# Two of four delta heads turned by VectorE and small stores in place of TensorE; output weights placed in attention's slots

## The chip, the cores and the metric

The kernel is one program on 1 core of one Trainium2 chip, launched once. Its time is the device time of that core in microseconds (us). Five engines work side by side, each through a queue of its own in a fixed order: PE (TensorE, matrix products; PEld is its weight load), DVE (VectorE), ACT (ScalarE), POOL (GpSimd) and SP (SyncE, which here issues nearly all DMAs). An instruction that waits holds everything behind it in its own queue.

## The reference, cut to what matters

One decoder block over 1024 tokens of width 1024, in float32: RMSNorm, one input projection, two groups of heads side by side, one output projection with the residual, and a last RMSNorm.

```python
h = rmsnorm(x, norm1_w)
proj = einsum('btd,de->bte', h, w_in)
sb_q, sb_k, sb_v, sb_z, g_q, g_k, g_v, g_z, g_b, g_a = split(proj)
o_sb = rmsnorm(stick_breaking_attention(sb_q, sb_k, sb_v)) * silu(sb_z)      # 8 heads of 64
qkv = silu(causal_depthwise_conv(concat([g_q, g_k, g_v]), conv_w))           # 4 taps
gq, gk, gv = split(qkv); gq = l2norm(gq); gk = l2norm(gk)                    # 4 heads of 128
o_gdn = gated_delta_chunked(gq, gk, gv, decay, beta)
o_gdn = rmsnorm(o_gdn) * silu(g_z)
x = x + einsum('bte,ed->btd', concat([o_sb, o_gdn]), w_out)
return rmsnorm(x, final_norm_w)
```

Stick-breaking attention weighs an earlier key s with sigmoid(z_ts) times the product of (1 - sigmoid) over the keys between. The gated delta rule works in chunks: inside a chunk a triangular system is solved, and a 128x128 state is carried from chunk to chunk (kernel: chunks of 128 tokens).

## The kernel before, in words

**Products.** Float32 accuracy comes from three products of split operands: each operand is a high part plus a low part (`xh`, `xl`; `weh`, `wel`; `woh`, `wol`; `mh`, `ml`), and `mm3` adds high x high, high x low, low x high. ScalarE makes the high part of a weight, GpSimd (for the output weights VectorE) the low part.

**Order.** The program isn't written in its order. Generators (streams) hand out pieces of work, and a model of the engines inside the builder (`Model`, with a `cost` for each instruction) decides at build time in which order each queue gets them; the five queues are then fixed. A DMA's cost in that model is a count of contiguous runs times a price per run. So an edit of one cost or one stream can move instructions in all queues.

**Stages.** Loads and the normalised input come first; then q of attention, half of v and the decays. Then the streams run together until about 520 us. `projections` goes through 16 column groups in the order G0 v1 k0 G1 k1 G2 k2 G3 k3 z4 to z7 z0 to z3: G is a delta head's k, q and v, z a gate. A group is 2 halves of 512 tokens with 24 products each; its products fill PE where the others leave room. `attention` goes through 8 heads with 4 windows each: products `pz<-kh,q`, sigmoids, a scan, `sgf` tiles, which PE transposes (`pz<-step,stf`), then `po<-ahl,v2a`. The windows' tiles lie in four fixed places, `sg0` to `sg3`.

**Delta heads.** `g_evac` takes a projected half of k (kind 1), q (kind 0) or v (kind 2): a copy to `pre`, four conv taps, sigmoid and product into `ac` (128 channels x 512 tokens), and a store to `g_s` in DRAM. `delta_load` loads k and q together as `kq` and v as `vt`, all with channels on the partitions. `gdn_pre` needs k, q and v with tokens on the partitions too: PE transposes them in blocks of 128x128 (`pz<-step,kwf`: k and q, 8 for each half of a head; `pz<-step,vt`: v, 4), ScalarE sums the squares of k and q (`nkv<-pz`), VectorE copies k to `kn`, ScalarE scales v into `nkv`. Then come the products of k with k and q (`pz<-kqf`), the triangular inverse (`gdn_sub`, `gdn_inv`) and the scan over chunks (`gdn_chain`), whose first product is `pc<-nkv,xinv`.

**Output.** When the delta heads are done, their pool is closed and the pool `f0` opened over it; eight row blocks of the output weights are loaded (`wor`) and split, the delta half (4 to 7) in `f0`, attention's half (0 to 3) in `f1` over the projection's pool. `enter_delta` and `enter_attention` load the mixed rows (`mgf`), `split` transposes and splits them (`mf`, `mh`, `ml`), and the last products go to `pp`.

**How to read names.** All instructions have line L358 (a helper records them), so rows are told apart by their tiles: out<-in. Numbers at the end of a tile are buffer numbers.

Of the kernel before, what the change touches and what calls it, by code (L numbers as in the profile page):

```python
# [28 lines left out]
ORDER = "G0 v1 k0 G1 k1 G2 k2 G3 k3 z4 z5 z6 z7 z0 z1 z2 z3".split()  # L29
LOADS = "k0 k1 x0 k2 x1 x2 k3 x3 x4 k4 x5 k5 x6 x7 k6 k7 c0 c1 c2 c3 s c4 c5 c6 c7".split()  # L30
WINDOWS = 3

# [360 lines left out]
def cost(eng, name, args, kw):  # L393

    size = lambda ap: int(np.prod(ap.shape[1:]))
    n = size(args[0])
    if eng == "S":
        run = min(contiguous(args[0]), contiguous(args[1]))
        return max(60, int(np.prod(args[0].shape)) * 4 / run * (10 + run / 21) / 16)
    if eng == "P":  # L400
        if name == "transpose":
            return 58 if args[1].dtype == F32R else 108
        n = size(args[2])
        if args[2].dtype == F32R:
# [69 lines left out]
def block(tc, xT_d, x_d, n1_d, wE_d, wQ_d, wC_d, conv_d, alog_d, dtb_d, mixw_d, wo_d, fnw_d, out_d):  # L474
# [4 lines left out]
    with ExitStack() as top:  # L479
# [391 lines left out]
        def g_evac(h, kind):  # L871
            wv = conv[:, 4 * kind + h, :]
            last = []

            def evac(pt, half):
                pre = gd.tile([P, 515], F32, tag="pre", bufs=2, name="pre")
                if half == 0:
                    V.memset(pre[:, 0:3], 0.0)
                else:
                    A.activation(pre[:, 0:3], last[0][:, 512:515], AF.Copy)  # L880
                last.append(pre)
                first(A.activation, pre[:, 3:515], pt, AF.Copy)
# [95 lines left out]
        def delta_load():  # L978
            yield lambda: "dec" in flags
            for h in range(GH):  # L980
                for g in range(2):
                    u = 2 * h + g
                    gst[h, g] = {}
                    half = "" if g else ".0"
                    yield lambda: u < 4 or f"c{u - 4}" in flags
                    if u > 3:
                        yield flags[f"c{u - 4}"]
                    kq = fx.tile([P, 4, 2, P], F32, "kq", "kq")
                    ts = slice(512 * g, 512 * g + 512)
# [4 lines left out]
                    gst[h, g].update(kq=kq)  # L994
                    flags[f"l{u}g"] = loads
                    yield lambda: f"G{h}2{half}" in flags and (u == 0 or f"q{u - 1}" in flags)
                    vt = gd.tile([P, 4, P], F32R, tag="vt", name="vt")
# [24 lines left out]
        def gdn_pre(h, g):  # L1022
            st = gst[h, g]
            kq = st["kq"]
            cs = slice(4 * g, 4 * g + 4)
            kn = gd.tile([P, 4, P], F32, tag="kn", bufs=4, name="kn")
# [6 lines left out]
            nkv = gd.tile([P, 4, P], F32, tag="nkv", bufs=4, name="nkv")  # L1033
            kw = fx.words(kq, "kw")
            for which in range(2):
# [5 lines left out]
                sq = [("A", 250)] * 4  # L1041
# [14 lines left out]
            G.tensor_scalar(qe, ss[:, 1, :], EPS * P, None, ALU.mult)  # L1056
            yield r
            nm = dt
            at = gd.tile([P, 4, P], F32, tag="at", bufs=4, name="at")
            for i in range(2):  # L1060
                gpt = pz()
                for j in range(2):
# [10 lines left out]
            flags[f"p{2 * h + g}"] = r  # L1073
            yield from until(f"v{2 * h + g}g")
            vt = st["vt"]
            tp = pz()
            for j in range(4):
                TE.transpose(tp[:, j * P:(j + 1) * P].bitcast(F32R), vt[:, j, :], idr)
            for j in range(4):
                A.activation(nkv[:, j, :], tp[:, j * P:(j + 1) * P], AF.Copy, scale=nk[:, j:j + 1])  # L1080
# [305 lines left out]
        wts = {}  # L1386
        pools = {}

        def weights_of(pool, ks, tag, bufs):
            ks = list(ks)  # L1390
            raws = {}

            def load(k):
                r = pool.tile([P, D], F32, tag=tag, bufs=bufs, name="wor")
                raws[k] = r, S.dma_start(r, wo_d[k * P:(k + 1) * P, :])

            for k in ks[:2]:
                load(k)
            for n, k in enumerate(ks):
                w, landed = raws[k]  # L1400
                yield landed
                wh, wl = [pool.tile([P, D], F32R, name=f"wo{c}{k}") for c in "hl"]
                A.activation(wh, w, AF.Copy, scale=mixw[:, k:k + 1])
                wts[k] = wh, wl, V.scalar_tensor_tensor(wl, w, mixw[:, k:k + 1], wh.bitcast(F32), ALU.mult, ALU.subtract)
                if n + 2 < len(ks):
                    load(ks[n + 2])

        def out_weights():
            yield lambda: "g" in flags
            gdn_ctx.close()  # L1410
            pools[0] = open_pool("f0", before=gd.ops())
            flags["pool0"] = True
            yield from weights_of(pools[0], range(4, 8), "xr", 3)

        def out_weights_attention():
# [4 lines left out]
            yield from weights_of(pools[1], range(4), "wr", 2)  # L1420
# [23 lines left out]
            return pools[0].tile([P, D], F32, tag="xr", bufs=3, name=name) if b < 3 else pools[1].tile([P, D], F32, tag="yr", bufs=5, name=name)  # L1444

        def enter_delta():
            yield lambda: "pool0" in flags and "z7" in flags and len(wts) > 1
            f0 = pools[0]
            for b in range(NB):
                yield lambda: fx.room("kq")  # L1450
# [82 lines left out]
        def products_attention():  # L1533
            yield lambda: f"d{NB - 1}" in flags
            for b in range(NB):
# [3 lines left out]
                for got in product(b, 0, parts):  # L1539
# [43 lines left out]
        pre = Stream(delta_pre(), 0.7, DELTA + 0.7)  # L1583
        interleave(ck, lambda: ps.room("pz", 4),
                   [Stream(delta_scan(), 0, DELTA), Stream(delta_solve(), 0.5, DELTA + 0.5), Stream(delta_substitute(), 0.6, DELTA + 0.6),
                    pre, Stream(delta_load(), 0.4, DELTA + 0.4), Stream(attention(), 9.995, WINDOW), Stream(attention_values(), 9.99, WINDOW), Stream(out_weights(), 9, OUT_WEIGHTS), Stream(out_weights_attention(), 9.25, OUTPUT + 1), Stream(enter_x(), 9.31, OUTPUT), fill,
                    Stream(enter_delta(), 9.3, OUTPUT), Stream(prepare(1), 9.2, OUTPUT), Stream(products_delta(), 101, OUTPUT),
                    Stream(enter_attention(), 9.1, OUTPUT - 3), Stream(prepare(0), 9.05, OUTPUT - 2), Stream(products_attention(), 102, OUTPUT - 1.5)])

# [37 lines left out]
```

## Time and profile before

| | |
|---|---|
| time, median of 3 runs | 645.64 us (645.34 to 646.01) |
| profiled execution, its own time | 647.36 us |
| its span (first to last instruction) | 645.0 us |
| TensorE's granted clock, mean | 0.998 |
| mean DMA rate over the span | 173 GB/s |

The span is shorter than the execution's own time, since starting and ending lie around it. The profile's page gives each engine's busy time and its share of the span, the chain of work that ended last, groups of instructions (count, busy us, mean ns of one, idle time of the engine before them and what ended it), and DMA issues (count, KB each, median us from issue to landing). Queries of the trace give the instructions in order of time (start us, length us), waits by engine (total us, times, longest), and busy times by window.

### The profile page before, as it was taken

What the parts mean: (1) busy time and instruction counts of PE and PEld (TensorE: products, weight loads), DVE (VectorE), ACT (ScalarE), POOL (GpSimd) and SP (SyncE); (2) the same over time, 40 slices, a digit from 0 to 9 for tenths busy, and PEclk for the clock granted to TensorE, in tenths of its full rate; (3) what the DMA queues carried; (4) which work ended last, traced back from release to release, by engine and by line L of the source; (5) the groups of instructions that cost most, each with busy time, mean ns of one, the idle gap of its engine ahead of it and who ended that gap; (6) DMA issues with size and microseconds to landing.
All of it is one profiled execution on the core that took longest, in us unless ns stands there. A gap on an engine that the chain in (4) does not pass through costs nothing.

```text
span 645.0 us, 11378 instructions
## 1 busy us (share of the span) xinstructions
PE 633.7 (98%) x3816; PEld 540.5 (84%) x3816; DVE 435.6 (68%) x810; ACT 392.6 (61%) x943; POOL 340.6 (53%) x429
## 2 busy tenths in 40 slices
PE   8999999999999999999999999999999999999996
PEld 7889988988888888888888788888888887888785
DVE  4359985133776797776877677667869527486874
ACT  5665467553876677856877766757578533222653
POOL 0125142964978487773569596477626131224742
PEclk9999999999999999999999999999999999999999
DMA  8968235886286352656254583444512259962323
GB/s 294 303 245 305 86 131 162 313 286 229 81 262 189 99 172 81 202 182 185 71 169 125 158 274 84 123 146 117 185 52 73 79 191 332 357 197 65 99 99 130
DMA packets 96633, 111.80 MB, mean 173 GB/s; under 512 B 28544, under 2 KB 61504, under 8 KB 96576
## 3 DMA queue, kind: packets, MB, share of 16 engines
q1 hardware_dynamic: 96288, 110.89, 52.2%
q8 instruction: 30, 0.49, 0.3%
q14 instruction: 27, 0.22, 0.1%
q10 hardware_dynamic: 288, 0.20, 0.1%
HBM read 76.03 MB, written 35.03 MB: 172 GB/s over the span
## 4 chain that ended last, share of the span: by engine, by line
PE 53%; POOL 3%; issue 2%; DVE 2%; DMA 1%; ACT 0%; POOLq 0%; SPq 0%
PE pp L358 34%; PE pz L358 13%; PE po L358 4%; PE pc L358 2%; DMA vt<-g_s 1%; POOL sgf L358 1%; POOL rsb L358 1%; POOL tt L358 0%; DVE xr L358 0%; POOL ac L358 0%; DVE cc L358 0%; POOL wel L358 0%; DVE ahl L358 0%; POOL ml L358 0%; POOL ry L358 0%
## 5 line engine op out<-in xcount | busy, mean ns | idle before, releaser
L358 PE MATMUL pp<-xh,weh 128*128 128x512 f32 x360 | 146.0, 406 | 0.0
L358 PE MATMUL pp<-xh,wel 128*128 128x512 f32 x360 | 141.2, 392 | 0.0
L358 PE MATMUL pp<-xl,weh 128*128 128x512 f32 x360 | 140.5, 390 | 0.0
L358 POOL TENSOR_TENSOR sgf<-sgf,cc 128x128 f32<-128x128 f32 (+3 forms) x64 | 77.3, 1210 | 48.0 <-DVE cc L358 46.7
L358 POOL TENSOR_TENSOR wel<-wer,weh 128x512 fp32r<-128x512 f32 x48 | 62.1, 1298 | 68.2 <-ACT weh L358 66.4
L358 PEld LDWEIGHTS pp<-xh,wel 128*128 128x128 f32 x360 | 67.5, 188 | 15.1
L358 PEld LDWEIGHTS pp<-xl,weh 128*128 128x128 f32 x360 | 67.8, 188 | 11.7
L358 PEld LDWEIGHTS pp<-xh,weh 128*128 128x128 f32 x360 | 67.7, 188 | 11.6
L358 DVE TENSOR_TENSOR_SCAN cc<-pz,step 128x384 f32<-128x384 f32 (+2 forms) x64 | 53.4, 847 | 13.7 <-ACT pz L358 7.5
L358 DVE TENSOR_TENSOR ahl<-pz,ahl 128x512 fp32r<-128x512 f32 (+1 forms) x80 | 50.0, 631 | 11.9 <-ACT ahl L358 11.5
L358 ACT ACTIVATE ahl<-pz 128x512 fp32r<-128x512 f32 (+1 forms) x80 | 44.0, 563 | 17.7 <-PE pz L358 17.4
L358 ACT ACTIVATE sgf<-pz,rs 128x384 f32<-128x384 f32 (+3 forms) x96 | 52.9, 593 | 1.5 <-PE pz L358 1.1
L358 PE MATMUL pp<-woh,mh 128*128 128x512 f32 (+2 forms) x132 | 52.1, 395 | 1.2 <-DVE xr L358 1.2
L358 ACT ACTIVATE pz<-pz,ns 128x384 f32<-128x384 f32 (+3 forms) x96 | 52.2, 577 | 0.0
L358 PE MATMUL pp<-woh,ml 128*128 128x512 f32 (+2 forms) x132 | 50.9, 385 | 0.0
L358 PE MATMUL pp<-wol,mh 128*128 128x512 f32 (+2 forms) x132 | 50.6, 384 | 0.0
L358 PE MATMUL po<-ahl,v2a 128*128 128x512 f32 (+1 forms) x160 | 49.0, 401 | 0.0
L358 POOL TENSOR_TENSOR ac<-ac,pre 128x512 f32<-128x512 f32 x24 | 30.9, 1291 | 30.8 <-ACT pre L358 24.2
L358 POOL TENSOR_TENSOR ml<-mf,mh 128x512 fp32r<-128x512 f32 x16 | 22.0, 1377 | 42.6 <-ACT mh L358 32.3
L358 DVE SCALAR_TENSOR_TENSOR pp<-pre,conv,pp 128x512 f32<-128x512 f32 x42 | 31.5, 749 | 18.3 <-ACT pp L358 18.0
L358 DVE TENSOR_TENSOR_SCAN cc<-pz,cc,step 128x512 f32<-128x512 f32 (+1 forms) x32 | 38.8, 1211 | 5.5 <-ACT pz L358 4.8
L358 PE MATMUL pz<-kh,q 128*128 128x384 f32 (+3 forms) x96 | 36.0, 381 | 0.2 <-DVE cc L358 0.2
(290 smaller groups left out, 1531.5 us busy)
## 6 DMA issues: line engine op xcount, KB each, us to landing
wer<-wE SPq DMA_DIRECT2D x48, 256.0 KB, 3.0
xr<-x SPq DMA_DIRECT2D x16, 512.0 KB, 7.4
g_s<-ac SPq DMA_DIRECT2D x24, 256.0 KB, 2.1
v_s<-v2e SPq DMA_DIRECT2D x16, 256.0 KB, 3.0
kqf<-g_s SPq DMA_DIRECT2D x16, 256.0 KB, 3.4
v2a<-v_s SPq DMA_DIRECT2D x8, 512.0 KB, 5.9
q<-qk_s SPq DMA_DIRECT2D x8, 512.0 KB, 4.0
kh<-qk_s SPq DMA_DIRECT2D x8, 512.0 KB, 3.9
```

The costliest lines, as they stand in the source:

```text
L358: ins = f(*args, **kw).ins
```

## The change

It has four parts.

1. For delta heads 2 and 3 (`h >= TURNED`), `g_evac` lets VectorE transpose the 128x512 result in blocks of 32x32 into the first 512 columns of `pre`, and stores that as four pieces of 32 partitions, in runs of 128 bytes, to a new array `gt_s`, whose rows are tokens. k and q are stored to `g_s` as well, v isn't.
2. For these heads `delta_load` loads `kn` (k), `nkv` (q) and `vt` (v) from `gt_s`, with tokens on the partitions; `gdn_pre` squares and scales from these tiles. PE's transposes and the copy to `kn` are left out. Heads 0 and 1 stay as they were.
3. The output weights' rows are loaded into the places `sg2` and `sg3`, two at a time, from attention's last windows on. Blocks 4 to 7 are split into attention's slots (`kh`, `kl`, `q2`, `cc`, `v2a`, `ahl`), blocks 0 to 3 in `f0`.
4. The builder's price for one DMA run of r bytes goes from 10 + r / 21 to 7.5 + r / 23.4 ns. This alone can move instructions anywhere.

```diff
+TURNED = 2
-        return max(60, int(np.prod(args[0].shape)) * 4 / run * (10 + run / 21) / 16)
+        return max(60, int(np.prod(args[0].shape)) * 4 / run * (7.5 + run / 23.4) / 16)
...
+        gt_s = dr.tile([GH, 3, T, P], F32, name="gt_s")
...
                 G.tensor_tensor(ac, ac, sg, ALU.mult)
-                return S.dma_start(g_s[h, kind, :, half * 512:half * 512 + 512], ac)
+                ts = slice(half * 512, half * 512 + 512)
+                if h < TURNED:
+                    return S.dma_start(g_s[h, kind, :, ts], ac)
+                done = [S.dma_start(g_s[h, kind, :, ts], ac)] if kind < 2 else []
+                first(V.transpose, sg, ac)
+                turned = gt_s[h, kind, ts, :].rearrange("(b r) d -> r b d", r=32)
+                return done + [S.dma_start(turned[:, :, 32 * a:32 * a + 32], sg[32 * a:32 * a + 32, :].rearrange("r (b c) -> r b c", c=32)) for a in range(4)]
...
+                    turned = lambda kind: gt_s[h, kind, ts, :].rearrange("(c t) d -> t c d", t=P)
+                    if h >= TURNED:
+                        loads += [S.dma_start(kn, turned(1)), S.dma_start(nkv, turned(0))]
...
-                    flags[f"v{u}g"] = S.dma_start(vt.rearrange("p c t -> p (c t)").bitcast(F32), g_s[h, 2, :, ts])
+                    vt = gd.tile([P, 4, P], F32 if h >= TURNED else F32R, tag="vt", name="vt")
+                    flags[f"v{u}g"] = S.dma_start(vt, turned(2)) if h >= TURNED else S.dma_start(vt.rearrange("p c t -> p (c t)").bitcast(F32), g_s[h, 2, :, ts])
...
+            for which, t in enumerate((kn, nkv)):
+                if h >= TURNED:
+                    for j in range(4):
+                        A.activation(at[:, j, :], t[:, j, :], AF.Square, accum_out=ss[:, which, j:j + 1])
+                    continue
                 tp = pz()
...
-            tp = pz()
+            tp = vt
+            if h < TURNED:
+                bank = pz()
+                tp = bank.rearrange("p (c t) -> p c t", c=4)
+                for j in range(4):
+                    TE.transpose(bank[:, j * P:(j + 1) * P].bitcast(F32R), vt[:, j, :], idr)
...
+        def out_rows():
+            yield lambda: f"s{SBH - 1}3" in flags and f"e{SBH - 1}1" in flags
+            for n, k in enumerate((4, 5, 6, 7, 0, 1, 2, 3)):
+                if n == 1:
+                    yield lambda: f"e{SBH - 1}2" in flags
+                if n > 1:
+                    yield lambda: fx.room(f"sg{1 + n % 2}")
+                r = fx.tile([P, D], F32, "wor", f"sg{1 + n % 2}")
...
         def out_weights():
+            places = [(t, 2 if t in ("cc", "ahl") else 1) for t in ("kh", "kl", "q2", "cc", "cc", "v2a", "ahl", "ahl")]
+            for n, k in enumerate(range(4, 8)):
+                yield lambda: k in raws and (n < 2 or f"e{SBH - 1}3" in flags)
+                yield raws[k][1]
+                weight(k, *[at_.tile([P, D], F32R, tag=t, bufs=m, name="wo") for t, m in places[2 * n:2 * n + 2]])
+                yield
```

What this does to the queues of PE and SP, at three places.

PE before, where head 3's first half of v stands (`pc<-xct`, `pz<-state` and `pz<-vr` are head 2's scan, `pz<-kh,q` and `otf` attention's):

```order
L358 MATMUL pz<-step,stf_4496 128x128 x3
L358 MATMUL pz<-kh,q_4072 128x512
L358 MATMUL pz<-kl,q_4072 128x512
L358 MATMUL pz<-step,vt 128x128 x4
L358 MATMUL pc<-xct,xinv 128x128
L358 MATMUL pz<-state,kqf_1992 128x128
L358 MATMUL pz<-vr,at 128x128
L358 MATMUL pz<-step,otf_4618 128x128 x2
```

A little ahead of it, PE before turns the same half head's k and q (`kwf_4406`; `stf` and `po` are attention's, `pz<-v_4389,kn` head 2's scan):

```order
L358 MATMUL po<-ahl,v2a 128x512 x3
L358 MATMUL po<-ahl,v2a 128x2x128
L358 MATMUL pz<-step,kwf_4406 128x128 x8
L358 MATMUL pz<-step,stf_4355 128x128 x3
L358 MATMUL pz<-v_4389,kn 128x128
```

PE in the change, where the same half head's k and q enter (`kqf_4204`):

```order
L359 MATMUL pp<-xl,weh 128x512
L359 MATMUL pp<-xh,wel 128x512
L359 MATMUL pc<-xct,xinv 128x128
L359 MATMUL pz<-kqf_4204 128x256 x4
L359 MATMUL pp<-xh,weh 128x512
```

Its products of k with k and q come without the eight transposes ahead of them, and no transpose of v follows for heads 2 and 3: 32 `kwf` and 16 `vt` rows are left of 64 and 32, with all other counts as before.

SP in the change, where head 2's first halves are stored and loaded (`ac` as before, `pre` turned; `xd`, `xe`, `xs`, `nb` belong to the triangular inverse):

```order
L359 DMA g_s<-ac 128x512
L359 DMA gt_s<-pre 32x16x32 x2
L359 DMA q_2869<-qk_s 128x1x1024
L359 DMA kh<-qk_s 128x1x1024
L359 DMA kl<-qk_s 128x1x1024
L359 DMA gt_s<-pre 32x16x32 x2
L359 DMA kqf_2909<-g_s 128x4x128
L359 DMA wer<-wE 128x512 x2
L359 DMA o_s<-oe 128x2x64
L359 DMA g_s<-ac 128x512
L359 DMA kn<-gt_s 128x4x128
```

Where a lone store stood before, four more follow it, and attention's loads and weight columns (`wer`) stand behind them.

SP before, around the last two loads of weight columns (group z3) and the first output rows:

```order
L358 DMA og_s<-goe 128x128 x3
L358 DMA gate_s<-zt 128x512
L358 DMA wer<-wE 128x512 x2
L358 DMA wor<-wo 128x1024 x2
L358 DMA gate_s<-zt 128x512
L358 DMA wor<-wo 128x1024
```

SP in the change, the same place (`worf` are output rows in `sg2` and `sg3`):

```order
L359 DMA worf_6481<-wo 128x1024
L359 DMA o_s<-oe 128x2x64
L359 DMA og_s<-goe 128x128
L359 DMA gate_s<-zt 128x512
L359 DMA og_s<-goe 128x128
L359 DMA mgf_6578<-og_s 128x512
L359 DMA worf_6619<-wo 128x1024
L359 DMA og_s<-goe 128x128
L359 DMA mgf_6578<-gate_s 128x4x128
L359 DMA worf_6634<-wo 128x1024
L359 DMA wer<-wE 128x512 x2
```

Three output rows and one block of mixed rows now stand ahead of z3's columns. `worf_6619` waits for PE's transposes of attention's last window and `worf_6634` for VectorE's split of the first row.

More of the change, by code (lines that the diff above doesn't have):

```diff
@@ L993, in delta_load @@
                         loads.append(S.dma_start(kq[:, :, 1 - kind, :], g_s[h, kind, :, ts].rearrange("p (c t) -> p c t", c=4)))
-                    gst[h, g].update(kq=kq)
+                    kn = gd.tile([P, 4, P], F32, tag="kn", bufs=4, name="kn")
+                    nkv = gd.tile([P, 4, P], F32, tag="nkv", bufs=4, name="nkv")
+                    gst[h, g].update(kq=kq, kn=kn, nkv=nkv)
+                    turned = lambda kind: gt_s[h, kind, ts, :].rearrange("(c t) d -> t c d", t=P)
+                    if h >= TURNED:
+                        loads += [S.dma_start(kn, turned(1)), S.dma_start(nkv, turned(0))]
                     flags[f"l{u}g"] = loads
                     yield lambda: f"G{h}2{half}" in flags and (u == 0 or f"q{u - 1}" in flags)
-                    vt = gd.tile([P, 4, P], F32R, tag="vt", name="vt")
-                    flags[f"v{u}g"] = S.dma_start(vt.rearrange("p c t -> p (c t)").bitcast(F32), g_s[h, 2, :, ts])
+                    vt = gd.tile([P, 4, P], F32 if h >= TURNED else F32R, tag="vt", name="vt")
+                    flags[f"v{u}g"] = S.dma_start(vt, turned(2)) if h >= TURNED else S.dma_start(vt.rearrange("p c t -> p (c t)").bitcast(F32), g_s[h, 2, :, ts])
                     gst[h, g].update(vt=vt)
@@ L1025, in gdn_pre @@
             cs = slice(4 * g, 4 * g + 4)
-            kn = gd.tile([P, 4, P], F32, tag="kn", bufs=4, name="kn")
+            kn, nkv = st["kn"], st["nkv"]
             ss = gd.tile([P, 2, 4], F32, tag="ss", name="ss")
@@ L1031, in gdn_pre @@
             S.dma_start(dt, dt_s[h, g])
-            nkv = gd.tile([P, 4, P], F32, tag="nkv", bufs=4, name="nkv")
+            at = gd.tile([P, 4, P], F32, tag="at", bufs=4, name="at")
             kw = fx.words(kq, "kw")
-            for which in range(2):
+            for which, t in enumerate((kn, nkv)):
[3 more added lines that the diff above has]
+                    continue
                 tp = pz()
@@ L1040, in gdn_pre @@
                     A.activation(nkv[:, j, :], tp[:, j * P:(j + 1) * P], AF.Square, accum_out=ss[:, which, j:j + 1])
-                sq = [("A", 250)] * 4
                 if which == 0:
@@ L1058, in gdn_pre @@
             nm = dt
-            at = gd.tile([P, 4, P], F32, tag="at", bufs=4, name="at")
             for i in range(2):
@@ L1075, in gdn_pre @@
             vt = st["vt"]
-            tp = pz()
+            tp = vt
[4 more added lines that the diff above has]
+                    TE.transpose(bank[:, j * P:(j + 1) * P].bitcast(F32R), vt[:, j, :], idr)
             for j in range(4):
-                TE.transpose(tp[:, j * P:(j + 1) * P].bitcast(F32R), vt[:, j, :], idr)
-            for j in range(4):
-                A.activation(nkv[:, j, :], tp[:, j * P:(j + 1) * P], AF.Copy, scale=nk[:, j:j + 1])
+                A.activation(nkv[:, j, :], tp[:, j, :], AF.Copy, scale=nk[:, j:j + 1])
             qg = kq[:, :, 1, :]
@@ L1387, in block @@
         pools = {}
[L1389 to L1394, printed above, removed]
-                raws[k] = r, S.dma_start(r, wo_d[k * P:(k + 1) * P, :])
[L1397 to L1406, printed above, removed]
@@ L1408, in out_weights @@
-        def out_weights():
+        raws = {}
+        def out_rows():
[6 more added lines that the diff above has]
+                r = fx.tile([P, D], F32, "wor", f"sg{1 + n % 2}")
+                ck.hold(r)
+                raws[k] = r, S.dma_start(r, wo_d[k * P:(k + 1) * P, :])
+                yield
@@ new lines, in weight @@
+        def weight(k, wh, wl):
+            w = raws[k][0]
+            A.activation(wh, w, AF.Copy, scale=mixw[:, k:k + 1])
+            wts[k] = wh, wl, V.scalar_tensor_tensor(wl, w, mixw[:, k:k + 1], wh.bitcast(F32), ALU.mult, ALU.subtract)
+            ck.free(w)
+        def out_weights():
+            places = [(t, 2 if t in ("cc", "ahl") else 1) for t in ("kh", "kl", "q2", "cc", "cc", "v2a", "ahl", "ahl")]
[3 more added lines that the diff above has]
+                weight(k, *[at_.tile([P, D], F32R, tag=t, bufs=m, name="wo") for t, m in places[2 * n:2 * n + 2]])
+                yield
@@ L1409, in out_weights, with out_weights_attention @@
+        def out_weights_attention():
             yield lambda: "g" in flags
             gdn_ctx.close()
-            pools[0] = open_pool("f0", before=gd.ops())
+            f0 = pools[0] = open_pool("f0", before=gd.ops())
             flags["pool0"] = True
-            yield from weights_of(pools[0], range(4, 8), "xr", 3)
-        def out_weights_attention():
+            for k in range(4):
+                yield lambda: k in raws
+                yield raws[k][1]
+                weight(k, *[f0.tile([P, D], F32R, name=f"wo{c}{k}") for c in "hl"])
+                yield
@@ L1416, in out_weights_attention, with out_rest @@
+        def out_rest():
             yield lambda: "proj" in flags and "pool0" in flags
@@ L1419, in out_weights_attention @@
             flags["pool1"] = True
-            yield from weights_of(pools[1], range(4), "wr", 2)
+            yield lambda: "d1" in flags
             fnw = wts["fnw"] = pools[1].tile([P, D], F32, name="fnw")
@@ L1446, in enter_delta @@
         def enter_delta():
-            yield lambda: "pool0" in flags and "z7" in flags and len(wts) > 1
+            yield lambda: "pool0" in flags and "z7" in flags
             f0 = pools[0]
@@ L1585, in block @@
                    [Stream(delta_scan(), 0, DELTA), Stream(delta_solve(), 0.5, DELTA + 0.5), Stream(delta_substitute(), 0.6, DELTA + 0.6),
-                    pre, Stream(delta_load(), 0.4, DELTA + 0.4), Stream(attention(), 9.995, WINDOW), Stream(attention_values(), 9.99, WINDOW), Stream(out_weights(), 9, OUT_WEIGHTS), Stream(out_weights_attention(), 9.25, OUTPUT + 1), Stream(enter_x(), 9.31, OUTPUT), fill,
+                    pre, Stream(delta_load(), 0.4, DELTA + 0.4), Stream(attention(), 9.995, WINDOW), Stream(attention_values(), 9.99, WINDOW), Stream(out_rows(), 9.1, OUT_WEIGHTS), Stream(out_weights(), 9, OUT_WEIGHTS), Stream(out_weights_attention(), 9.25, OUTPUT + 1), Stream(out_rest(), 9.26, OUTPUT + 1), Stream(enter_x(), 9.31, OUTPUT), fill,
                     Stream(enter_delta(), 9.3, OUTPUT), Stream(prepare(1), 9.2, OUTPUT), Stream(products_delta(), 101, OUTPUT),
```

## The prediction

> **What bounds the kernel now.** I read the page's busy line first, then PE's waits, its instructions in order of time, and its groups by form.
>
> ```profile
> span 645.0 us, 11378 instructions
> PE 633.7 (98%) x3816; PEld 540.5 (84%) x3816; DVE 435.6 (68%) x810; ACT 392.6 (61%) x943; POOL 340.6 (53%) x429
> PE 53%; POOL 3%; issue 2%; DVE 2%; DMA 1%; ACT 0%; POOLq 0%; SPq 0%
> ...
> PE po L358 <- DVE step L358: 1.7, 1, 1.7
> PE pz L358 <- DMA vt<-g_s: 1.3, 1, 1.3
> PE pp L358 <- DVE xr L358: 1.2, 2, 0.8
> PE pz L358 <- DVE cc L358: 0.5, 2, 0.3
> ...
> 638.34 0.28 PE L358 MATMUL pp<-woh,ml 128*128 128x192 f32 x1
> ```
>
> PE is busy for 98% of the span, and the chain that ends last runs through it. It waits 4.7 us in all: 1.7 us before its first product, and 3.0 us (1.3 + 1.2 + 0.5) later. Its last product ends at 638.6 us, so 6.4 us of 645.0 lie behind it. In between PE has work nearly without a break: a microsecond taken out of its queue should come out of the time, and each new wait costs its full length.
>
> How much queue an instruction takes is not its duration, since matmuls overlap. It is the distance from one start to the next:
>
> ```profile
> L358 PE MATMUL pz<-step,kwf 128*128 128x128 f32 x64 | 6.9, 247 | 0.0
> L358 PE MATMUL pz<-step,vt 128*128 128x128 f32 x32 | 4.5, 265 | 1.3 <-DMA vt<-g_s 1.3
> ...
> 353.27 0.80 PE L358 MATMUL pz<-step,kwf 128*128 128x128 f32 x8
> 353.91 0.42 PE L358 MATMUL pz<-step,stf 128*128 128x128 f32 x3
> ...
> 291.02 0.65 PE L358 MATMUL pz<-step,vt 128*128 128x128 f32 x4
> 291.50 0.34 PE L358 MATMUL pz<-step,otf 128*128 128x128 f32 x2
> ...
> 365.65 0.40 PE L358 MATMUL pz<-kl,q 128*128 128x512 f32 x1
> 367.33 0.51 PE L358 MATMUL pz<-step,vt 128*128 128x128 f32 x4 [1.29 <-DMA vt<-g_s]
> 367.68 0.46 PE L358 MATMUL pc<-xct,xinv 128*128 128x128 f32 x2
> ```
>
> The first two rows are groups by form (busy us, mean ns, idle before them), the others stand in order of time (start, length). A transpose of k or q lasts 247 ns, but eight of them (a half head) take 353.91 - 353.27 = 0.64 us of queue, 80 ns each. Four of v take 0.48 us at 291.02 and 0.35 us at 367.33.
>
> **The change, part by part.** (1) TensorE's transposes go for heads 2 and 3: 32 of the 64 kwf rows (k, q) and 16 of the 32 vt rows. That is 4 x 0.64 = 2.56 us and 4 x 0.42 (between 0.35 and 0.48) = 1.68 us, together **4.2 us**. At least 4.2 - 3.0 = 1.2 us of it must show, if each wait above only stood behind transposes; at most all of it does.
>
> (2) PE's wait for v goes. The seventh of the eight v groups, head 3's first half, stood at the head of PE's queue from 366.04 (367.33 - 1.29) while its load was under way:
>
> ```profile
> 360.48 0.45 SPq L358 DMA_DIRECT2D vt<-g_s  x1
> ...
> 478.83 0.38 PE L358 MATMUL pc<-nkv,xinv 128*128 128x128 f32 x2
> ```
>
> In the change ScalarE reads that tile itself. Next late would be nkv, which it makes of v; head 3's scan wants that at 478.83, some 110 us later. So **1.3 us** more, between 0 and 1.3, if nothing takes its place.
>
> (3) VectorE loses four copies of kn and gains twelve transposes of 128x512; ScalarE reads squares and v from SBUF instead of PSUM.
>
> ```profile
> L358 DVE COPY kn<-pz 128x512 f32<-128x512 f32 x8 | 5.5, 691 | 6.8 <-ACT nkv L358 6.8
> L358 DVE STREAM_TRANSPOSE wc<-xc 128x256 f32<-128x256 f32 x4 | 1.7, 430 | 0.0
> ...
> L358 ACT ACTIVATE ahl<-pz 128x512 fp32r<-128x512 f32 x48 | 28.4, 602 | 10.9 <-PE pz L358 10.7
> L358 ACT ACTIVATE weh<-wer 128x512 fp32r<-128x512 f32 x48 | 30.6, 639 | 7.0 <-POOL wel L358 2.3 <-PE pp L358 2.1 <-PE pz L358 1.2
> ...
> core 0: us, PE busy (x) PEld busy (x) DVE busy (x) ACT busy (x) POOL busy (x), PEclk, DMA share, GB/s
> 220.00:350.00 130.00, 129.69 (x841) 110.45 (x841) 100.62 (x191) 95.21 (x252) 89.02 (x125) 1.00 0.49 150
> ```
>
> A 128x512 transpose isn't in the trace; it lies between 430 ns (half its size) and 860 (twice that), and I take the copy's 0.7 us. That adds 12 x 0.7 - 4 x 0.69 = 5.6 us to a VectorE that is idle for 29 of the 130 us in which heads 2 and 3 are projected. ScalarE pays some 37 ns (639 - 602) on 48 instructions, 1.8 us, with 35 us idle. Both lie beside PE: nothing, and 7 us if that cover were gone.
>
> (4) Each of twelve half heads now stores four pieces of 32x16x32, runs of 128 bytes. Four of them replace one v store, and kn and nkv add eight loads: 44 + 8 = 52 more issues on SP. The nearest row is bd, the stretch in which four bd stores have the engines to themselves:
>
> ```profile
> L358 SPq DMA_DIRECT2D bd<-dt x32: 303/428/680, 138.1 to 402.4; - x32
> ...
> DMA packets 285, 0.03 MB, mean 25 GB/s; under 512 B 285, under 2 KB 285, under 8 KB 285
> ...
> q1 hardware_dynamic: 285, 0.03, 17.7%
> ...
> bd<-dt SPq DMA_DIRECT2D x4, 16.0 KB, 1.4
> ...
> q1 hardware_dynamic: 21572, 19.35, 48.3%
> ```
>
> SP spends 52 x 0.43 = 22 us more issuing. Behind a store that waits for VectorE stand loads of weight columns and attention's q and k, which are issued ahead of their use by about one half head (12.7 us, under 5). In that stretch (1.3 us long) 285 packets took 17.7% of 16 engines: 0.177 x 16 x 1300 / 285 = 12.9 ns each. So 12 x 2048 packets of 128 bytes are 12 x 2048 x 12.9 / 16 = 20 us of all engines. For the loads I add at most 15 us: 8 x 256 KB at the small packets' rate (128 bytes in 12.9 ns on 16 engines, 159 GB/s) are 13 us, and the vt loads cut to 512-byte runs 2 us. Between 220 and 350 us the engines are 48.3% busy (the last row above): 67 us are free, and 35 fit. Forecast: nothing.
>
> [...]
>
> (5) The stores read the first 512 columns of pre, one of two buffers, which is so held for longer.
>
> ```profile
> L358 ACT ACTIVATE pre<-pp x12: 597/598/652, 217.3 to 357.4; 128x512 f32<-128x512 f32 x12
> ...
> L358 ACT ACTIVATE pre<-ac x12: 630/634/708, 223.3 to 363.2; 128x512 f32<-128x512 f32 x12
> ```
>
> The first of these to the second is 6.0 us of evacuation; sigmoid and product add 0.6 + 1.3, the transpose 0.7, four issues 1.7, a landing 2.0: 12.3 us. Half heads of 2 and 3 come every (357.4 - 217.3) / 11 = 12.7 us, and two buffers allow twice that: covered.
>
> (6) The eight rows of output weights are loaded when attention's last windows leave their tiles; four are split into attention's slots. The splits are the same work. But SP now has three row loads ahead of the last weight columns (z3), the second of which waits for PE's last big group of attention transposes.
>
> ```profile
> 528.00 0.39 PE L358 MATMUL pp<-xl,weh 128*128 128x512 f32 x1
> 528.23 0.39 PE L358 MATMUL pp<-xh,wel 128*128 128x512 f32 x1
> ...
> 520.00:560.00 40.00, 39.22 (x186) 32.10 (x185) 20.94 (x40) 14.60 (x24) 10.90 (x10) 1.00 0.91 323
> ...
> wer<-wE SPq DMA_DIRECT2D x48, 256.0 KB, 3.0
> ...
> wor<-wo SPq DMA_DIRECT2D x8, 512.0 KB, 4.2
> ...
> mgf<-og_s SPq DMA_DIRECT2D x8, 256.0 KB, 7.2
> ...
> L358 POOL TENSOR_TENSOR wel<-wer,weh 128x512 fp32r<-128x512 f32 x48 | 62.1, 1298 | 68.2 <-ACT weh L358 66.4
> ```
>
> From those transposes on: six issues at 0.4 = 2.4, landing 3.0, weh 0.64, wel 1.3: 7.3 us until z3 can run. PE has 42 products of z2 before that (0.23 us from start to start: 9.7) and a few of attention's, 11 us. That leaves 3.7 us. At the 7.2 us of the mgf loads in the same burst (engines 91% busy from 520 to 560 us) z3 would be late by about 0.5 us.
>
> **The sum.** 4.2 + 1.3 = 5.5 us off. The whole order is rewritten, and I expect new waits of about the size of the old ones that I can't place: I take 1.0 us for (6) and for them. Net -4.5 us. The profiled execution, 647.4 with its span of 645.0 and 2.4 around it, becomes 642.9 with a span of 640.5; the median shown, 645.64, becomes **641.1 us**.
>
> **The rivals.** *The saving is eaten by new waits (same).* Place (6) has 3.7 us to spare by median landings; one more row load of 4.2 us in front of z3's columns at crowded landings (0.5 late already) makes 4.7 us of waiting, which undoes 4.5: 645.8. Half of that gives 643.5. For it: the engines are 91% busy there, and the delta heads' work moves in the queues too. Against: PE waits 3.0 us behind its start in a program of the same kind. Time 643.2 to 647.
>
> *The small stores fill the DMA engines (slower).* They take 1.54 us per ns that a packet costs (12 x 2048 / 16). With 67 - 15 = 52 us free, it decides from 34 ns a packet; beyond it columns land late and PE stands. At 40 ns that is 9.4 us, net +3.9: 649.5 us. Against it: the 12.9 ns of bd, from a stretch in which bd was alone. [...]
>
> *PE isn't full (same).* Weight loads keep PEld busy for 84%, so if products and loads overlapped freely, 48 transposes would fit beside the rest and their removal would bring nothing: 645.6. Against: the transposes' starts follow at 80 ns while each of their weight loads lasts 140, so loads overlap one another and 84% is no measure of room.
>
> ```profile
> L358 PEld LDWEIGHTS pz<-step,kwf x64: 138/140/146, 111.0 to 389.9; 128*128 128x128 f32 x64
> ```
>
> [...]
>
> *More than forecast.* All 5.5 us and the two waits for xr (1.2): 638.9.
>
> That the change does not do what it says is excluded by the order: 48 transposes are missing there.
>
> **How the numbers follow.** Forecast (638.9 to 643.2): 0.67. Eaten: 0.17, a third of it still under 644.35. DMA engines full: 0.07. PE not full: 0.04. More: 0.05. About 0.2% (1.3 us) is what a measurement of this kernel can tell from no change. Faster: 0.67 + 0.05 + 0.06 = 0.78. Slower: 0.07 + 0.03 of the eaten case = 0.10. Same: 0.12. The range goes from 638.6 to 646.0, which leaves out the full engines, the upper end of the eaten case and little below.
>
> **What would show it.** PE's groups: kwf x32, vt x16, other counts unchanged; PE's busy time down by more than 4 us (durations overlap). In PE's waits no vt; a wait for POOL wel or a DMA of wer around 515 to 530 us speaks for the first rival. The DMA share between 220 and 350 us should be about 0.75; at 0.95, with PE waiting for wel, the second is right. VectorE's transposes at about 0.7 us. If PE's last product doesn't end earlier although the transposes are gone and no wait is listed, the third is right. I would be wrong if waits of more than 3 us in sum appear anywhere in PE's queue.

## The result, and the profile after

| | before | after |
|---|---|---|
| time, median | 645.72 us (6 runs, 645.34 to 646.01) | 641.99 us (6 runs, 641.69 to 642.58) |
| ratio after / before, 95% interval | | 0.9941 (0.9931 to 0.9950) |
| profiled execution, its span | 647.36, 645.0 us | 641.73, 639.8 us |

The change is faster by 3.7 us; 641.1 was forecast. The busy lines, the shares of the chain and the main DMA queue on the page of after:

```profile
span 639.8 us, 11363 instructions
PE 630.5 (99%) x3768; PEld 536.1 (84%) x3768; DVE 443.1 (69%) x818; ACT 394.3 (62%) x945; POOL 340.3 (53%) x429
q1 hardware_dynamic: 126816, 115.09, 57.0%
PE 90%; DVE 3%; ACT 3%; POOL 1%; DMA 1%; issue 1%; POOLq 0%; DVEq 0%; ACTq 0%; SPq 0%
```

PE has 48 instructions fewer (3768 for 3816) and is busier in share. Its waits in after (total us, times, longest):

```profile
PE po L359 <- DVE step L359: 1.7, 1, 1.7
PE pp L359 <- DVE v2e L359: 0.4, 1, 0.4
PE pz L359 <- DVE dt L359: 0.2, 1, 0.2
```

The wait at the start stays; 0.6 us are left beside it, where the profile of before had 3.0. No wait for a weight column or for q, k or v is among them. The groups by form, and busy times by window (PE, PEld, DVE, ACT, POOL, granted clock, DMA share, GB/s):

```profile
L359 PE MATMUL pz<-step,kwf 128*128 128x128 f32 x32 | 3.4, 246 | 0.0
L359 PE MATMUL pz<-step,vt 128*128 128x128 f32 x16 | 2.2, 263 | 0.0
L359 DVE STREAM_TRANSPOSE pre<-ac 128x512 f32<-128x512 f32 x12 | 8.5, 707 | 5.4 <-POOL ac L359 5.4
L359 DVE COPY kn<-pz 128x512 f32<-128x512 f32 x4 | 2.7, 685 | 5.1 <-ACT nkv L359 5.1
...
220.00:350.00 130.00, 129.95 (x795) 110.16 (x793) 102.54 (x187) 93.46 (x257) 91.81 (x136) 1.00 0.67 181
520.00:560.00 40.00, 40.00 (x191) 32.78 (x190) 26.17 (x54) 13.87 (x19) 10.82 (x8) 1.00 0.94 335
```

The transposes of two heads are gone, VectorE's twelve took 0.71 us each, and in the two windows PE is busy for 129.95 us of 130 and for all 40. The question is then how much of the 3.7 us is the shorter queue, how much the new order, and how near the other engines came to their limits.

### The profile page after: what moved, and what is told of

Same layout as the page of the kernel before. It is cut to its first block, busy times and chain, and to the rows that moved or that the text cites. A ratio compares the mean times of both kernels' runs of the same rounds, so it can differ in the third digit from the quotient of the medians.

```text
span 639.8 us, 11363 instructions
## 1 busy us (share of the span) xinstructions
PE 630.5 (99%) x3768; PEld 536.1 (84%) x3768; DVE 443.1 (69%) x818; ACT 394.3 (62%) x945; POOL 340.3 (53%) x429
## 4 chain that ended last, share of the span: by engine, by line
PE 90%; DVE 3%; ACT 3%; POOL 1%; DMA 1%; issue 1%; POOLq 0%; DVEq 0%; ACTq 0%; SPq 0%
PE pp L359 54%; PE pz L359 25%; PE po L359 7%; PE pc L359 3%; DMA cb<-cum_s 1%; DVE cc L359 1%; DVE pp L359 1%; ACT pre L359 1%; DMA n<-n 1%; ACT pz L359 0%; POOL ac L359 0%; DVE ahl L359 0%; POOL dt L359 0%; DVE ac L359 0%; ACT sgf L359 0%
## 5 line engine op out<-in xcount | busy, mean ns | idle before, releaser
L359 PE MATMUL pp<-wo,mh 128*128 128x512 f32 x128 | 40.7, 399 | 0.0
L359 PEld LDWEIGHTS pz<-step,stf 128*128 128x128 f32 x288 | 30.8, 141 | 5.5 <-DVE cc L359 0.6
L359 ACT ACTIVATE weh<-wer 128x512 fp32r<-128x512 f32 x48 | 30.4, 636 | 5.8 <-PE pp L359 2.6
```

The costliest lines, as they stand in the source:

```text
L359: ins = f(*args, **kw).ins
```

## The experiments

Each kernel ran on one chip beside the kernel before, whose medians there were 645.74 to 645.82 us. The change's own six runs (641.99 us) were taken beside 645.72.

### Is it the length of PE's queue?

**put_back** is the change with the 48 transposes issued again, in the change's order on every queue.

```diff
             gpt = pz()
+            if h >= TURNED:
+                for n in range(6):
+                    nc.tensor.transpose(gpt[:, n % 4 * P:n % 4 * P + P].bitcast(F32R), kw[:, 2 * i + n % 2, n // 2 % 2, :], idr)
```

They stand eight times, six ahead of each group of products of k with k and q, which overwrites what they leave.

> The changed kernel with 48 transposes of k and q put back into TensorE's queue ahead of the delta products of heads 2 and 3 (their result is overwritten and not used); every other instruction and every queue's order is as in the changed kernel, 641.99 us. Theory (TensorE's queue length is what counts, 80 to 88 ns a transpose): 4.0 us slower, 646.0 (645.2 to 646.8), the whole gain gone. Rival (the gain comes from the new order, the price table and where the output weights lie): within 1 us of 642.0.

Measured: 645.61 us (11 runs, 645.42 to 645.99), ratio to before 1.0000 (0.9991 to 1.0008). Its busy line and its waits:

```profile
PE 634.1 (99%) x3816; PEld 539.5 (84%) x3816; DVE 444.6 (69%) x818; ACT 394.2 (61%) x945; POOL 340.1 (53%) x429
...
PE po L359 <- DVE step L359: 1.7, 1, 1.7
PE pp L359 <- DVE v2e L359: 0.6, 1, 0.6
```

No wait came with them; the time is that of the kernel before. So 48 transposes are worth 645.61 - 641.99 = 3.62 us, 75 ns each, and by this measure the rest of the change (stores, VectorE's transposes, ScalarE's new operands, output weights, order) nets to 3.73 - 3.62 = 0.1 us. The rival "PE isn't full" falls: weight loads are busy for 84%, and still each transpose counts.

**before_again** is a second profiled execution of the kernel before.

> The kernel before once more, for a second profile. If the 1.3 us wait of TensorE for v belongs to the kernel, this profile lists it again at about 366 us, 1.0 to 1.6 us long. If it belonged to that one execution (its own time, 647.36, lay 1.6 above the median), the wait is under 0.3 us or not listed, and the span is about 643.5.

It took 645.20 us. Its waits of PE, the place where the first profile showed the wait for v, and SP's issues ahead of it:

```profile
PE po L358 <- DVE step L358: 1.7, 1, 1.7
PE pp L358 <- DVE xr L358: 1.2, 2, 0.8
PE pz L358 <- DVE cc L358: 0.5, 2, 0.3
...
365.23 0.40 PE L358 MATMUL pz<-kl,q 128*128 128x512 f32 x1
365.46 0.46 PE L358 MATMUL pz<-step,vt 128*128 128x128 f32 x4
...
360.62 0.42 SPq L358 DMA_DIRECT2D vt<-g_s  x1
```

Here v is turned 0.23 us after the product ahead of it starts, without a wait. The 1.3 us belonged to the profiled execution of 647.36 us, which was 1.35 us above the slowest of the six runs behind the median.

### The parts alone

**price_alone** is the kernel before with the new price of a DMA run (part 4); **not_turned** is the change with `TURNED = 4`, so parts 3 and 4 only; **old_price** is the change with the old price, parts 1 to 3; **old_place** is the change with the output weights where they were, parts 1, 2 and 4 (its PE queue is the change's up to the last windows of attention).

```diff
-        return max(60, int(np.prod(args[0].shape)) * 4 / run * (10 + run / 21) / 16)
+        return max(60, int(np.prod(args[0].shape)) * 4 / run * (7.5 + run / 23.4) / 16)
...
-TURNED = 2
+TURNED = 4
```

The first edit is price_alone's on the kernel before (old_price takes it back on the change), the second not_turned's.

> The kernel before with the builder's price of a DMA run alone changed (7.5 + run / 23.4 in place of 10 + run / 21): same instructions, other order. Theory: the order alone is worth little, 645.7 within 1.5 us (644.2 to 647.2). Rival (the order brings the gain): 642 to 643.

> The changed kernel with no head turned by VectorE (TURNED = 4): new price and the new places of the output weights, TensorE's 48 transposes back. Theory: 4.2 us slower than the changed kernel apart from chance in the order: 646.2 (644.7 to 647.7). Rival (output weights' places and price bring the gain): 642 to 643.

> The change with the builder's old price of a DMA run (10 + run / 21), so that the work is the same and only the queues' orders differ. Theory (the gain is the length of PE's queue, and the new price brings nothing by itself): within 1 us of the change, 641 to 643. Rival (the new price is needed so that the many small stores are planned well): 643.5 or more, with waits of PE over 1.5 us in its list, in the stretch from 220 to 400 us or behind 500 us.

> The turning of heads 2 and 3 and the new price, with the output weights loaded and split where they were before. PE's queue is the change's, row for row, up to the last windows of attention (about 500 us). Theory (the place of the output weights brings nothing but what PE waits for there): up to 500 us the same as the change; behind it the wait for xr (1.2 us in the kernel before) comes back, 642 to 643.5 us. Rival 1 (the new place is what gains, the turning only pays for it): 645 or more. Rival 2 (the new place costs, three row loads ahead of the last weight columns): 641.5 or less.

| kernel | parts | median us (range, runs) | ratio to before (95%) |
|---|---|---|---|
| price_alone | 4 | 649.39 (648.07 to 653.16, 6) | 1.0063 (1.0044 to 1.0081) |
| not_turned | 3, 4 | 650.41 (648.89 to 651.14, 5) | 1.0073 (1.0060 to 1.0086) |
| old_price | 1, 2, 3 | 647.06 (646.25 to 649.09, 10) | 1.0021 (1.0012 to 1.0031) |
| old_place | 1, 2, 4 | 641.57 (641.46 to 641.63, 3; a fourth took 792.24 at a granted clock of 0.727, cause unknown) | 0.9933 (0.9913 to 0.9953) |

None of the four came out as its theory said. old_place (642 to 643.5 expected) is no slower than the change, so part 3 brings nothing that can be measured, and parts 1, 2 and 4 together carry the whole gain. The wait for xr came back with 0.5 us instead of 1.2. The other three are too slow: a new order without the turning costs 3.6 and 4.7 us, and the turning in the old price's order is 5 us slower than in the new, as old_price's rival had it (643.5 or more). The work is the same in each pair, so the order makes the difference. In not_turned and old_price (first and second block, PE's waits over 0.5 us behind the start):

```profile
PE pp L359 <- POOL wel L359: 1.3, 1, 1.3
PE pz L359 <- issue: 1.1, 1, 1.1
PE pp L359 <- DVE v2e L359: 0.6, 1, 0.6
...
PE pp L359 <- issue: 1.6, 1, 1.6
PE pp L359 <- POOL wel L359: 1.1, 1, 1.1
PE pp L359 <- POOL ml L359: 0.6, 1, 0.6
```

These waits are only a part of it. All waits behind the start come to 3.6 us in not_turned and 1.7 in before_again, with 3.7 us between the two profiled executions; in old_price they come to 3.7 us and in the change to 0.6, with 4.7 us between those. Where the rest is lost isn't shown.

### What such a wait is made of

price_alone's profiled execution was the slowest of its six (653.16). PE's worst wait in it, what VectorE did ahead of it (start, length; `x2` joins two copies), the group of these copies (min/median/max), and GpSimd's instructions in that time:

```profile
379.08 0.40 PE L358 MATMUL pp<-xh,wel 128*128 128x512 f32 x1
383.09 1.35 PE L358 MATMUL pz<-xc,y 32*32 32x32 f32 x29 [3.62 <-issue]
...
376.32 5.80 DVE L358 COPY wy<-wc 32x256 f32<-32x256 f32 x2
382.13 0.86 DVE L358 COPY y<-pz 32x256 f32<-32x256 f32 x2
...
L358 DVE COPY wy<-wc x8: 274/484/4774, 192.4 to 464.3; 32x256 f32<-32x256 f32 x8
...
377.13 0.67 POOL L358 MEMSET xinv<- 64x512 f32 x1
377.76 1.76 POOL L358 TENSOR_TENSOR sgf<-sgf,cc 128x896 f32<-128x896 f32 x1
379.49 1.26 POOL L358 TENSOR_TENSOR wel<-wer,weh 128x512 fp32r<-128x512 f32 x1
380.71 1.26 POOL L358 TENSOR_TENSOR kqf<-kqf,cb 128x512 f32<-128x512 f32 x1
```

A copy from SBUF to SBUF, 274 ns at its shortest here, took 4,774 and ended at 382.12, with the last of four GpSimd instructions that followed one another (380.71 + 1.26 = 381.97). `y<-pz` stood behind it on VectorE, and PE behind that. This is the slowest execution; how long the copy took in the other five (648.07 to 649.55) isn't known.

**price_summed** is price_alone in its own order, with only these eight copies made by a sum over an axis of length one; **after_summed** does the same to the change.

```diff
-            V.tensor_copy(W[0:32, :, 0:32], wc[0:32])
+            nc.vector.tensor_reduce(W[0:32, :, 0:32], wc[0:32].rearrange("p c (i u) -> p c i u", u=1), AX.X, ALU.add)
```

The second copy of each pair is replaced alike.

> price_alone in its own order, in which only the eight VectorE copies of 32x256 from wc to wy are made by another instruction (a sum over an axis of length one). In price_alone one of these copies lasted 4,774 ns instead of about 280, from 377.34 to 382.12 us, as long as GpSimd ran products one behind the other; PE waited 3.6 us right behind it, and its next products of 128x512 started 0.43 us apart instead of 0.23. Theory (the copy is held up by GpSimd, and that makes price_alone slow): all eight last under 500 ns, PE's wait of 3.6 us is gone, and so is the slow stretch behind it (another 2 to 3 us); 649.4 - 3.6 to 6.5 = 643 to 646 us. Rival (the wait belongs to the chain of the inverse as such, or any VectorE instruction would be held up): wy still lasts over 1 us there or PE still waits more than 2 us, 648 to 650.

> The change in its own order, with the same eight copies made by the other instruction. In the change they are held up as well (8 copies: 270 to 1,773 ns, 5.4 us above their shortest in sum), but PE lists no wait behind them. Theory (only what PE waits for counts): wy under 500 ns and the time within 0.6 us of the change, 641.4 to 642.6. Rival (VectorE's lost 5 us cost something): more than 1 us faster than the change, under 641.

price_summed: 646.65 us (10 runs, 645.48 to 647.00), 2.7 us below price_alone. The group, and PE's waits over 0.5 us:

```profile
L359 DVE TENSOR_REDUCE wy<-wc x8: 377/402/410, 191.3 to 456.6; 32x256 f32<-32x256 f32 x8
...
PE po L361 <- DVE step L361: 1.7, 1, 1.7
PE pp L361 <- POOL wel L361: 1.3, 1, 1.3
```

All eight last about 0.4 us, with GpSimd busy for 7.65 us of the 10 from 370 to 380 us (6.83 in price_alone), and the wait of 3.6 us is gone; the one for wel stays. So the length of this copy is what made most of price_alone's loss of 3.6 us. What makes the 0.8 us that price_summed still loses isn't shown. after_summed took 641.85 us (4 runs, 641.67 to 642.24) against 641.99: in the change's own order the same copies take up to 1,773 ns too, but nothing that PE wants stands behind them, and freeing them brings nothing.

### More heads, fewer heads

**turned3**, **turned1** and **turned0** are the change with `TURNED` 3, 1 and 0: one, three and four heads turned.

> The change with only head 3 turned; 24 transposes come back to TensorE. Theory (length of PE's queue): 24 x 75 = 1.8 us more than the change, 643.8 us. Rival (order decides, and turning head 2 matters through the waits it avoids at 355 to 390 us): waits in PE's list like those of not_turned (POOL wel 1.3, issue about 1 or more there), time 646 or above.

> The change with head 1 turned as well (three heads instead of two); 24 more of TensorE's transposes leave its queue. Theory (time follows the length of PE's queue; put_back gave 75 ns for each transpose): 24 x 75 = 1.8 us less than the change, 640.2 us; PE's waits beside the one at the start stay under 1 us. Rival (the order decides: price_alone and not_turned moved by 3.6 and 4.7 us with the same work in another order): a wait of 1 us or more appears in PE's list, and the time stands above 641.5 by about its length. Rival 2 (128-byte stores fill the DMA engines): 36,864 packets, share over the span up from 57% to about 62%, and PE waits for wel.

> The change with all four heads turned; no transpose of k, q and v is left on TensorE. Theory (length of PE's queue): 48 x 75 = 3.6 us less than the change, 638.4 us, no new wait of PE over 1 us. Rival (order decides): waits in PE's list above 1 us, time above 640. Rival 2 (small stores): DMA share over the span about 66%, PE waits for wel or for a DMA, time at or above 642.

| heads turned | 1 (turned3) | 2 (change) | 3 (turned1) | 4 (turned0) |
|---|---|---|---|---|
| by PE's queue alone, us | 643.8 | 641.99 | 640.2 | 638.4 |
| measured, us | 649.32 | 641.99 | 646.45 | 655.20 |
| range, runs | 647.72 to 650.04, 4 | 641.69 to 642.58, 6 | 645.00 to 648.56, 10 | 653.73 to 655.47, 4 |

All three fall to "the order decides". The rival of full DMA engines expected waits for wel in turned1 and turned0, and none is listed; but short stretches of full engines do play a part, as turned1 shows below. turned3's longest wait behind the start, 1.5 us for a load of mixed rows (`mgf<-gate_s`), is none of those that were expected. turned1's longest wait shows the turning's own price; PE, ScalarE and SP there (SP: the four stores of one turned tile, `x3` joins three), and a window of it:

```profile
194.78 0.50 PE L359 MATMUL pp<-xh,weh 128*128 128x512 f32 x1 [3.03 <-DVE ac L359]
...
190.38 0.60 ACT L359 ACTIVATE pre<-pp 128x512 f32<-128x512 f32 x1 [2.76 <-DMA gt_s<-pre]
...
178.29 1.46 SPq L359 DMA_DIRECT2D gt_s<-pre  x3
184.58 0.53 SPq L359 DMA_DIRECT2D gt_s<-pre  x1
...
196.00:198.00 2.00, 2.00 (x12) 1.60 (x10) 2.00 (x4) 2.00 (x16) 2.00 (x3) 0.50 0.56 107
```

Three stores are issued from 178.29, the fourth only at 184.58, behind loads of attention's q and k and of kqf. It lands some 5.8 us after that (the median of turned1's 72 such stores is 2.4), with the DMA engines' share at 0.93 to 1.11 from 184 to 190 us. Until then the `pre` buffer isn't free; ScalarE waits 2.8 us to evacuate the next half head into it, so `ac` is late and the PSUM bank that PE wants is still full. turned0's list has a wait of 1.5 us for `ac` as well, beside others up to 2.2 us. Whether a third buffer would cure turned1 wasn't tried.

### How much room the stores have

**stores_twice** is the change in its own order, with each of the 48 small stores issued a second time.

```diff
+                for a in range(4):
+                    done[a - 4].again = nc.sync.dma_start(*piece(gu_s, a)).ins
```

`piece` gives the addresses of the store to `gt_s`, behind which each of these stands in SP's queue.

> The change in its own order, with each of its 48 stores of 128-byte runs issued a second time right behind the first, to an array that nothing reads: 24,576 more packets and 48 more issues on SP (48 x 0.43 = 21 us of its queue). The turned tile (pre) is held for longer too. Theory (stores, issues and held buffer lie beside PE with room): DMA share between 220 and 350 us up from 0.67 by 0.1 to 0.15, no new wait of PE over 1 us, time within 1 us of the change, 641 to 643. Rival (the small stores are close to filling the engines or SP's queue): PE waits for wel, for q and k of attention or for ac, time 645 or more.

Measured: 652.42 us (4 runs, 651.28 to 656.08), 10.4 above the change: the theory missed by far. The rival's time (645 or more) came in, though PE waits for none of the tiles that it named. Its window, PE's waits, the place of the longest on SP, VectorE and PE, and last the same load on SP in the change:

```profile
220.00:350.00 130.00, 127.67 (x771) 107.66 (x770) 100.97 (x181) 89.59 (x236) 89.16 (x133) 0.99 0.73 185
...
PE pz L359 <- DVE dt L359: 3.7, 1, 3.7
PE pz L359 <- ACT pz L359: 2.3, 1, 2.3
...
356.30 0.43 SPq L359 DMA_DIRECT2D dt<-dt_s  x1
...
362.07 0.76 DVE L359 TENSOR_TENSOR at<-pz,dt 128x256 f32<-128x256 f32 x2 [3.31 <-DMA dt<-dt_s]
...
363.49 0.46 PE L359 MATMUL pz<-v,kn 128*128 128x128 f32 x2 [3.65 <-DVE dt L359]
...
346.73 0.43 SPq L359 DMA_DIRECT2D dt<-dt_s  x1
```

Two things stand in this wait. SP issued one DMA after another, and `dt<-dt_s` came out at 356.30, 9.6 us later than in the change (346.73), of which PE's own lateness by then explains some 4 (the products of k with k and q ahead of the wait start at 356.55 for 352.28). It then took 5.8 us to land, and held VectorE and then PE. The DMA share of 0.73 (0.67 in the change) is an average: in the windows of 2 us from 358 to 364, while that load was under way, it was 1.01, 1.04 and 1.05. The change has such windows too (1.09 from 352 to 354), with a wait of 0.2 us for `dt` behind them. The other wait (2.3 us) is ScalarE waiting for a `pre` buffer, as in turned1.

So late issues, held buffers and stretches of full engines come together here, and how much each costs isn't separated: a run that adds packets without issues wasn't made.

## Why the prediction was right, step by step

The direction, the range and the mechanism held: the gain is the shorter PE queue. Its sizes and covers, one by one:

- **(1) The transposes, 4.2 us.** 3.62 us by put_back: 75 ns each, where I took 80 for k and q and 105 for v. put_back's 48 are all of k and q, so v's own size stays open. By another measure the term was nearly right: summed from start to start over PE's rows, kwf and vt take 5.36 and 3.18 us in before_again, 2.59 and 1.58 in the change, 4.4 us less. So what the rest of the change adds or takes is known to some 0.8 us only.
- **(2) The wait for v, 1.3 us.** This step failed. The wait was read from one execution of 647.36 us and subtracted from a median that hadn't got it; before_again has no such wait.
- **(3) VectorE and ScalarE beside PE: nothing.** Right: 0.707 us for 0.7 predicted, and of PE's waits behind the start only the 0.2 us for `dt` has one of these transposes shortly ahead of it on VectorE.
- **(4) Issues and packets: nothing.** Right in result, wrong in what it rested on. The DMA share became 0.67 (0.75 forecast), but the margin I reckoned with, 34 ns a packet before the engines fill, was one of averages over 130 us. Summed over SP's rows between 220 and 350 us, issues took 46 us before and 77 after: 31 us more, where 22 were reckoned. Doubling the stores cost 10 us at a mean share of 0.73, by late issues and in stretches in which the engines were full.
- **(5) The `pre` buffer, 12.3 us of 25: covered.** Right for heads 2 and 3, but too wide a margin: the step left out that other DMAs stand between the four stores, and took 2.0 us for a landing that in turned1 took some 5.8. stores_twice and turned1 wait exactly there.
- **(6) Output rows ahead of z3's columns.** No wait there; old_place shows no gain from the new place either.
- **The allowance of 1.0 us for new waits.** It covered most of the error of step (2): 4.2 + 1.3 - 1.0 = 4.5 against 3.7 measured. That the forecast came within 0.9 us of the median is so far luck. The waits behind the start did not grow but fell, from 1.7 us in before_again to 0.6 in the change, and that brought nothing to be seen: put_back lists 0.6 us too and is no faster than the kernel before. Where that 1.1 us went isn't shown.

One sign that the prediction named missed: PE's busy time fell by 3.2 us (633.7 to 630.5), not by more than 4. PE's last product ends at 633.2 us, where it ended at 638.6 in the first profile of before and at 636.7 in before_again.

Of the rivals, "the saving is eaten by new waits" didn't happen, yet the runs show how near it was: old_price, turned3 and turned0 do the same kind of work in other orders and lose more than they save, and turned1 loses about as much (ratio 1.0012, 0.9999 to 1.0024). That the order of the change is nearly free of such waits is shown; why the builder's model found a good one at two heads and the new price, and not beside it, stays open.

## What to carry to other kernels

Where PE has work without a break, look at the start-to-start distance of what leaves its queue and not at the weight loads' share: here 48 transposes paid 75 ns each at a share of 84%. Put them back in the frozen order to see that it is they. With a builder that rewrites all queues, change one thing in a frozen order before believing in a part's worth: orders here differ by 3.6 to 5.1 us with the same work. Moving work from PE to small DMAs was paid in the issuing queue (31 us more of SP between 220 and 350 us) and in buffers held until the last piece landed (in turned1 12 us from the issue of the first, 178.29, to ScalarE's next use at 190.38). Reckon these as well as the DMA engines' share, and take that share at the place of the wait, not as an average. Read a wait off a second profiled execution before counting on it.

## What the runs showed of the hardware

**A VectorE copy waited out a train of GpSimd instructions.** 274 ns became 4,774 beside four of them in price_alone, where the copy ended 0.15 us behind the last (382.12 and 381.97). In the change five of the eight copies took 987 to 1,773 ns, each to 0.14 or 0.15 us behind the end of the GpSimd product that ran when it started (279.97 behind 279.83, for one); the other three took 270 to 285 ns, one of them (457.81 to 458.08) beside such a product as well. A sum over an axis of one, doing the same, took 377 to 410 ns in price_alone's order and 386 to 409 in the change's. Why the copy waits and the sum doesn't isn't shown.

**Some of PE's long waits were paid a second time, at a granted clock of 0.50.** Behind turned1's wait of 3.03 us the granted clock is 0.50 (the window quoted above) and 0.82 in the windows of 2 us on both sides of it, and products of 128x512 start 0.43 us apart instead of 0.23: some 1.7 us lost, an estimate from these three windows. In price_alone it is down to 0.50 behind 3.62 us; behind old_price's 1.65 us it stays at 1.00. That profiled run of old_price is one of five that took 646.25 to 646.46 us at a mean granted clock of 0.997 to 0.998; the other five took 647.65 to 649.09 at 0.993 to 0.995, and no trace shows where in them the clock was lower. The length of the wait alone doesn't tell the cases apart, as two places of turned0 show (PE, then the window behind it):

```profile
546.28 0.60 PE L359 MATMUL pz<-step,mwf 128*128 128x128 f32 x3 [2.00 <-DVE mgf L359]
548.00:550.00 2.00, 1.19 (x2) 0.50 (x2) 2.00 (x2) 0.45 (x1) 1.47 (x1) 0.50 1.03 352
...
128.07 0.50 PE L359 MATMUL pp<-chl,xh 128*128 128x256 f32 x2 [2.24 <-DVE v2e L359]
130.00:132.00 2.00, 2.00 (x20) 2.00 (x19) 1.38 (x5) 0.39 (x1) 1.27 (x1) 1.00 0.99 261
```

Behind 2.00 us the clock was 0.50, behind 2.24 us 1.00. What makes the difference isn't shown.
